# A decoder block's last row tiles: the row tile ahead of the last scaled on ScalarE and GpSimd instead of VectorE

## The chip, the core and the metric

The kernel runs on one core of a Trainium2 chip. Its time is the device time of one execution, in microseconds (us). A core has five engines with an in-order instruction stream each: TensorE (PE, matrix products into PSUM banks), VectorE (DVE), ScalarE (ACT), GpSimd (POOL) and SyncE (SP, which mostly issues DMA transfers). Engines meet only through semaphores. "Span" is the time from the first to the last instruction of the profiled execution.

## What is computed

One layer of a decoder block over 1024 tokens of width 1024, in float32: a mixer (a gated recurrence and a pooling branch), a layer norm, a squared-ReLU MLP and a second layer norm. Only the end matters here:

```python
x = layer_norm(DEEPNORM_ALPHA * x + mixer(x), ln1_g, ln1_b)
x = layer_norm(DEEPNORM_ALPHA * x + square(relu(x @ w_up)) @ w_down, ln2_g, ln2_b)

def layer_norm(x, g, b):
    mu  = mean(x);  var = mean(square(x - mu))
    return (x - mu) * rsqrt(var + 1e-5) * g + b
```

## The kernel before

A row tile is 128 tokens by 1024 features, and there are eight, numbered 0 to 7. Every float32 operand is split into a high and a low part, and each product is three matmuls (lines 1279 to 1281). The MLP's second product uses a Strassen-like scheme: seven products of half-size blocks, each added into one half (512 features) of four row tiles by `add_to` on VectorE (line 1235), which reads a PSUM bank and adds to the row tile `r[t]` in SBUF.

In the last block of the loop, the product `p5` completes row tiles 4 to 7, and after each of them `last_norm(t)` is called. The last two products, `p3` and `p2`, complete row tiles 0 to 3, and are issued interleaved by a list written out by hand, `(0, 0), (0, 1), (1, 0), (0, 2), (1, 1), (1, 2), (0, 3), (1, 3)`: first the product, then the row tile. So row tile 3 (`CH - 1`, with `CH` = 4) is the last to be finished, and row tile 2 (`CH - 2`) the one ahead of it. The adds and statistics of row tile 3 are given a higher priority. The order in which each engine's instructions finally stand is made by a scheduler at build time; the order in the source is only its input.

`last_norm(t)` works in four steps, and each line of it becomes one instruction, or one per half:

- statistics. For every row tile but the last, ScalarE sums the row (1307), turns the sum into minus the mean (1308), sums the squares around it (1309) and takes the root (1310). For row tile 3, VectorE's `bn_stats` (1042) runs after each half, then `bn_aggr` (1303), and ScalarE only takes the root (1304).
- first pass on VectorE (1315): `(r + minus mean) * g2`, in place.
- reciprocal of the root on VectorE, 128x1 (1316).
- second pass on VectorE (1318): `r * rstd + b2`, in place, then the DMA to the output (1319).

`parts` holds the slices that the passes run over: the whole row of 1024 for row tiles 0 to 2 and 4 to 7, two halves of 512 for row tile 3. The second `for` pairs each slice with a queue, the first with SP, the second with ScalarE's; with a whole row only SP is used. `g2` and `b2` are the norm's gain and bias, copied to all 128 partitions in SBUF (names `ln` in the profile); `mv` (name `lmv`) holds mean, root and reciprocal. Row tiles appear as `act` and, for row tile 7, `y`. GpSimd has issued the loads of the row tiles (1289) and computes nothing in this stage; its last elementwise work on whole row tiles is the bias add of the first layer norm (1062).

Of the kernel before, what the change touches and what calls it, by code (L numbers as in the profile page):

```python
# [12 lines left out]
AF = mybir.ActivationFunctionType  # L13
# [3 lines left out]
P = 128  # L17
# [6 lines left out]
CH = HALF // P  # L24
# [18 lines left out]
def tile_hybrid_block(  # L43
# [18 lines left out]
    nc = tc.nc  # L62
    V, A, G, PE = nc.vector, nc.scalar, nc.gpsimd, nc.tensor
    x2, out2 = x[0], out[0]
# [15 lines left out]
    def nm(s):  # L80
        seq[0] += 1
        return f"{s}_{seq[0]}"
# [38 lines left out]
    def split_into(t, src):  # L121
# [9 lines left out]
        out=cmask, in_=cmask, compare_op=ALU.is_ge, fill=0.0, base=0,  # L131
# [14 lines left out]
    r = [None] * 8  # L146
# [252 lines left out]
    with tc.tile_pool(name="xr", bufs=8, side="right", reuse_waits="tile") as xr:  # L399
# [68 lines left out]
        def parts(rows):  # L468
            return [split(row, row_tile) for row in rows]
# [62 lines left out]
        w = parts(b11)  # L532
        first_tokens("a12", "tr")
        onto_chain(w, "a11", True, copied(c11, c_late))
        with behind_parts("a11"):
            w = parts(b21)
        second_tokens("s3", "tr")
        by_rows(w, "a12", take_p2)
        with behind_parts("a12"):
            for k in range(CH):  # L540
                V.tensor_sub(b22[k], b22[k], b12[k])
            w = parts(b22)
# [3 lines left out]
        with behind_parts("s3"):  # L546
# [3 lines left out]
            w = parts(b21)  # L550
        second_tokens("s2")
        by_rows(w, "a22", take_p4)
        with behind_parts("a22"):
            w = parts(b22)
# [3 lines left out]
        with tc.issue_after(taken["a22", 1]):  # L558
            for k in range(CH):
                V.tensor_sub(b12[k], b12[k], b11[k])  # L560
            w = parts(b12)
# [7 lines left out]
        with behind_parts("s1"):  # L569
            w = parts(b22)  # L570
# [470 lines left out]
    def stats(t, cc, st):  # L1041
        V.bn_stats(st[:, cc], t[:, cc * HALF : (cc + 1) * HALF])
# [21 lines left out]
    def stat_tile():  # L1064
        return stat.tile([P, 2, 6], F32, tag="lst", name=nm("lst"), bufs=8)

    def ln_params(tile_of, *srcs):
        out = []
        for src in srcs:
            out.append(tile_of())  # L1070
            nc.scalar.dma_start(out=out[-1], in_=src.to_broadcast([P, D]))
        return out
# [5 lines left out]
    with tc.tile_pool(name="wo", bufs=1, side="right", reuse_waits="tile") as mp:  # L1078
        st1 = [None] * 8
        g1, b1 = ln_params(lambda: f(act_tile()).rearrange("p a b -> p (a b)"), ln1_g, ln1_b)  # L1080
        for k2 in range(0, KT, 2):
            raw = raw_rows(w_out, k2, 1)
            for k in range(2):
                n = len(wo)
# [47 lines left out]
    with tc.tile_pool(name="up", bufs=1, side="right", reuse_waits="tile") as up:  # L1132
# [96 lines left out]
        def add_to(t, n, ps):  # L1229
            y = r[t][:, n * HALF : (n + 1) * HALF]  # L1230
            if (t, n) not in touched:
                V.scalar_tensor_tensor(y, y, ALPHA, ps, ALU.mult, ALU.add)
                touched.add((t, n))
            else:
                V.tensor_add(y, y, ps)
# [38 lines left out]
        def down_tile(ops, chain, fresh, c):  # L1274
            ps = banks[1 - chain][c]
            w = slice(c * P, (c + 1) * P)
            for n in range(M):
                hh, hl, wh, wl = (t[:, n % 2] for t in ops[n // 2])
                PE.matmul(ps, hh[:, w], wh, start=fresh and n == 0, stop=False, skip_group_check=True)  # L1279
                PE.matmul(ps, hh[:, w], wl, start=False, stop=False, skip_group_check=True)  # L1280
                PE.matmul(ps, hl[:, w], wh, start=False, stop=n == M - 1, skip_group_check=True)  # L1281
            return ps
# [13 lines left out]
        for c, ps in done:  # L1296
            add_to(c, nh, ps)

    def last_norm(t):

        mv = stat.tile([P, 4], F32, tag="lmv", name=nm("lmv"), bufs=4)
        if t == CH - 1:
            V.bn_aggr(mv[:, 0:2], st1[t])
            A.activation(mv[:, 2:3], mv[:, 1:2], AF.Sqrt, bias=eps_ln)
        else:
            junk = dr.tile([P, D], F32, tag="junk", name=nm("junk"))
            A.activation(junk, r[t], AF.Copy, accum_out=mv[:, 3:4])
            A.activation(mv[:, 0:1], mv[:, 3:4], AF.Copy, scale=-1.0 / D)
            A.activation(junk, r[t], AF.Square, bias=mv[:, 0:1], accum_out=mv[:, 1:2])
            A.activation(mv[:, 2:3], mv[:, 1:2], AF.Sqrt, bias=eps_ln, scale=1.0 / D)  # L1310
        n = 2 if t == CH - 1 else 1
        parts = [slice(i, i + D // n) for i in range(0, D, D // n)]
        for w in parts:
            op = ALU.subtract if t == CH - 1 else ALU.add
            V.scalar_tensor_tensor(r[t][:, w], r[t][:, w], mv[:, 0:1], g2[:, w], op, ALU.mult)
        V.reciprocal(mv[:, 2:3], mv[:, 2:3])
        for w, eng in zip(parts, (nc.sync, nc.scalar)):
            V.scalar_tensor_tensor(r[t][:, w], r[t][:, w], mv[:, 2:3], b2[:, w], ALU.mult, ALU.add)
            eng.dma_start(out=out2[t * P : (t + 1) * P, w], in_=r[t][:, w])
# [5 lines left out]
    for b in range(NBLK):  # L1325
        if b:
            ws = ws_nxt
        last = b == NBLK - 1
        if last:

            for ring in (dh, dw):
                t = fw.tile([P, M, 2, HALF], F32R, tag="draw", name=nm("dx"), bufs=2)
                ring[:0] = [(t[:, n], t[:, n + 1]) for n in (0, 2)]
        for i, (name, slot, chain, fresh, (u, nh)) in enumerate(steps):
            if b == 0 and i == 0:
                continue
            if i == 2 and not last:
                ws_nxt = [(fw if b % 2 else dr).tile([P, M, D], F32, tag="draw", name=nm("draw"), bufs=2) for _ in range(2)]
                draws = down_rows(b + 1, ws_nxt)
            if i > 2 and not last and draws:  # L1340
                draws.pop(0)(h_load[0])
            if i == 2 and last:
                g2, b2 = ln_params(lambda: dr.tile([P, D], F32, tag="ln", name=nm("ln"), bufs=2), ln2_g, ln2_b)
            if last and name == "p3":
                break
            if b or i > 1:
                ops = down_operands(b, name, slot)
            for c in range(CH):
                t = u * CH + c
                add_to(t, nh, down_tile(ops, chain, fresh, c))  # L1350
                if last and name == "p5":
                    last_norm(t)
# [4 lines left out]
    for i, c in ((0, 0), (0, 1), (1, 0), (0, 2), (1, 1), (1, 2), (0, 3), (1, 3)):  # L1357
        _, _, chain, fresh, (_, nh) = ends[i]
        ps = down_tile(ops[i], chain, fresh, c)
        with tc.high_priority(PRIO) if c == CH - 1 else nullcontext():  # L1360
            add_to(c, nh, ps)
            if c == CH - 1:
                st1[c] = st1[c] if i else stat_tile()
                stats(r[c], nh, st1[c])
            if i:
                last_norm(c)


# [29 lines left out]
```

## Time and profile before

| what | value |
|---|---|
| time, median of 3 runs | 1460.14 us (1459.37 to 1463.32) |
| the profiled execution: its own time | 1462.62 us |
| the profiled execution: span | 1460.9 us |
| busy: DVE, ACT, POOL | 1137.3, 755.2, 60.5 us |
| last matmul starts | 1451.45 us |
| output issues after the last matmul | 1457.2 us (SP), 1457.91 us (ScalarE) |

Times in the profile are counted from the start of the span. Some 1.7 us of the profiled execution's own time lie outside its span. In a row of the timeline the columns are start, duration, engine, line, operation, output and inputs by name, shapes, and in brackets the idle time of the engine ahead of it with what ended it. In such a row the duration includes the drain of the pipeline, so the next instruction of the engine can start a little before the end. All times of this text refer to the kernel's line numbers before the change unless "changed kernel" is said; a suffix such as "row 2" means row tile 2.

### The profile page before, as it was taken

How to read it: one execution, taken by the hardware profiler on the slowest of the kernel's cores; microseconds unless marked ns; L12 is line 12 of the kernel's file. 1: busy time of each engine (PE TensorE's matmuls, PEld its weight loads, DVE VectorE, ACT ScalarE, POOL GpSimd, SP SyncE). 2: the span in 40 equal slices, each digit the busy share in tenths (PEclk: the TensorE clock that was granted, in tenths of full speed). 3: DMA queues.
4: the chain of work that ended last, by engine and by line, in shares of the span. 5: the costliest groups of instructions: out<-in, count | busy, mean ns of one | idle time of the engine just before them, and what ended most of it. 6: DMA issues, size and time to landing. Idle time of an engine off the chain costs nothing.

```text
span 1460.9 us, 20889 instructions
## 1 busy us (share of the span) xinstructions
PE 1438.2 (98%) x7505; PEld 1187.2 (81%) x7505; DVE 1137.3 (78%) x1838; ACT 755.2 (52%) x1381; POOL 60.5 (4%) x244
## 2 busy tenths in 40 slices
PE   9999999999999999999999999999999999999997
PEld 7888888888887887877788878888888888888886
DVE  5968989899997785768985597666666787777977
ACT  5545565665666566455442376555555443333535
POOL 0002010001001010000002100000000100000000
PEclk9999999999999999999999999999999999999999
DMA  7232233223333447987563225445464874444422
GB/s 252 77 118 88 85 104 114 82 94 103 103 121 116 152 133 236 334 285 249 193 224 119 73 94 195 146 141 170 142 242 155 288 260 152 151 137 167 129 72 116
DMA packets 160616, 226.84 MB, mean 155 GB/s; under 512 B 11232, under 2 KB 84480, under 8 KB 160512
## 3 DMA queue, kind: packets, MB, share of 16 engines
q1 hardware_dynamic: 158576, 218.93, 44.8%
q0 software_dynamic: 1152, 4.19, 0.9%
q10 hardware_dynamic: 784, 2.38, 0.5%
q8 instruction: 59, 0.97, 0.3%
q14 instruction: 45, 0.37, 0.1%
HBM read 154.16 MB, written 71.30 MB: 154 GB/s over the span
## 4 chain that ended last, share of the span: by engine, by line
PE 83%; DVE 7%; DMA 5%; ACT 3%; issue 2%; SPq 0%; DVEq 0%; ACTq 0%
PE ps_pj L199 14%; PE ps_pj L200 14%; PE ps_pj L201 14%; PE ps_pj L1280 4%; PE ps_pj L1281 4%; PE ps_pj L1279 4%; PE ps_pj L104 2%; PE ps_pj L105 2%; PE ps_pj L106 2%; DVE w L118 1%; PE ps_tr L1281 1%; PE ps_tr L1280 1%; PE ps_tr L1279 1%; PE ps_sc L199 1%; DMA draw<-in_w_down_dram 1%
## 5 line engine op out<-in xcount | busy, mean ns | idle before, releaser
L199 PE MATMUL ps_pj<-act,w 128*128 128x512 f32 x1068 | 419.8, 395 | 6.1 <-ACT w L117 3.1
L200 PE MATMUL ps_pj<-act,w 128*128 128x512 f32 x1068 | 417.7, 391 | 0.5 <-DVE act L123 0.5
L201 PE MATMUL ps_pj<-act,w 128*128 128x512 f32 x1068 | 412.0, 392 | 0.1
L199 PEld LDWEIGHTS ps_pj<-act,w 128*128 128x128 f32 x1068 | 200.8, 188 | 51.0 <-ACT w L117 4.9
L201 PEld LDWEIGHTS ps_pj<-act,w 128*128 128x128 f32 x1068 | 200.9, 188 | 43.2 <-DVE w L118 1.1
L200 PEld LDWEIGHTS ps_pj<-act,w 128*128 128x128 f32 x1068 | 201.1, 188 | 41.2 <-DVE act L123 0.9
L117 ACT CAST w<-t 128x512 fp32r<-128x512 f32 x170 | 104.9, 620 | 115.6 <-PE ps_pj L200 59.9
L118 DVE TENSOR_TENSOR w<-raw,w 128x512 fp32r<-128x512 f32 x143 | 99.1, 698 | 57.8 <-ACT w L117 43.7
L118 DVE TENSOR_TENSOR w<-t,w 128x512 fp32r<-128x512 f32 x170 | 115.9, 684 | 29.2 <-ACT w L117 27.5
L117 ACT CAST w<-raw 128x512 fp32r<-128x512 f32 x143 | 88.1, 620 | 89.4 <-PE ps_pj L200 39.7
L1241 ACT CAST act<-act 128x1024 fp32r<-128x1024 f32 x66 | 67.0, 1051 | 111.5 <-PE ps_pj L1280 36.1
L1280 PE MATMUL ps_pj<-act,act 128*128 128x512 f32 x240 | 93.3, 390 | 0.3 <-DVE act L1242 0.3
L1281 PE MATMUL ps_pj<-act,act 128*128 128x512 f32 x240 | 93.1, 389 | 0.0
L1279 PE MATMUL ps_pj<-act,act 128*128 128x512 f32 x240 | 92.4, 389 | 0.0
L1242 DVE TENSOR_TENSOR act<-act,act 128x1024 fp32r<-128x1024 f32 x66 | 79.3, 1219 | 16.1 <-ACT act L1241 16.0
L272 DVE TENSOR_TENSOR c<-c,ps_pj 128x512 f32<-128x512 f32 x95 | 64.5, 679 | 31.9 <-PE ps_pj L201 29.7
L268 ACT COPY c<-ps_pj 128x512 f32<-128x512 f32 x96 | 55.4, 584 | 15.4 <-PE ps_pj L201 14.8
L814 DVE RECIPROCAL tC<-tA 128x128 f32<-128x128 f32 x64 | 54.6, 906 | 0.0
L1280 PEld LDWEIGHTS ps_pj<-act,act 128*128 128x128 f32 x240 | 45.0, 188 | 10.1 <-DVE act L1242 0.7
L1279 PEld LDWEIGHTS ps_pj<-act,act 128*128 128x128 f32 x240 | 45.0, 188 | 9.4
L1281 PEld LDWEIGHTS ps_pj<-act,act 128*128 128x128 f32 x240 | 45.1, 188 | 9.2
L238 DVE TENSOR_TENSOR t<-raw,raw 128x512 f32<-128x512 f32 x43 | 29.5, 687 | 15.7 <-DMA raw<-in_w_in_dram 12.9
(415 smaller groups left out, 2721.0 us busy)
## 6 DMA issues: line engine op xcount, KB each, us to landing
h<-c SPq DMA_DIRECT2D x106, 256.0 KB, 2.3
act<-h SPq DMA_DIRECT2D x78, 256.0 KB, 3.0
raw<-in_w_in_dram SPq DMA_DIRECT2D x64, 256.0 KB, 3.4
draw<-in_w_down_dram SPq DMA_DIRECT2D x16, 1024.0 KB, 7.6
raw<-in_w_up_dram SPq DMA_DIRECT2D x30, 512.0 KB, 4.2
raw<-in_w_in_dram SPq DMA_DIRECT2D x18, 512.0 KB, 3.9
hf<-h SPq DMA_DIRECT2D x34, 256.0 KB, 2.9
c<-o SPq DMA_DIRECT2D x24, 256.0 KB, 4.2
```

Source lines behind the costliest of these rows:

```text
L117: A.copy(hi, src)
L118: V.tensor_sub(lo, src, f(hi))
L199: PE.matmul(ps, wh[:, k], th, start=first and k == 0, stop=False, skip_group_check=True)
L200: PE.matmul(ps, wh[:, k], tl, start=False, stop=False, skip_group_check=True)
L201: PE.matmul(ps, wl[:, k], th, start=False, stop=k == CH - 1, skip_group_check=True)
L268: A.copy(t, ps)
L272: V.tensor_add(t, t, ps)
L1241: A.copy(hi, src)
L1242: V.tensor_sub(lo, src, f(hi))
L1279: PE.matmul(ps, hh[:, w], wh, start=fresh and n == 0, stop=False, skip_group_check=True)
L1280: PE.matmul(ps, hh[:, w], wl, start=False, stop=False, skip_group_check=True)
L1281: PE.matmul(ps, hl[:, w], wh, start=False, stop=n == M - 1, skip_group_check=True)
```

## The change

Row tile 2 gets a path of its own inside `last_norm`. Its statistics stay. VectorE takes the reciprocal; ScalarE computes minus the mean times the reciprocal (128x1) and then, in two halves of 512, `r * rstd + that` in place; GpSimd multiplies each half by `g2`; GpSimd adds `b2` to the first half, and VectorE adds `b2` to the second. That last add is kept back in the list `ends_of` and issued behind the last call of `last_norm`. Both halves are sent from SP's queue.

The test for two parts is now `t >= CH - 2`. `last_norm` is also called for row tiles 4 to 7, so these too run in halves: eight passes of 1024 become sixteen of 512, and the second half of each of the four is sent from ScalarE's queue. Row tiles 0 and 1 stay whole, row tile 3 stays as it was.

```diff
+    ends_of = []
+
     def last_norm(t):
...
-        n = 2 if t == CH - 1 else 1
+        n = 2 if t >= CH - 2 else 1
         parts = [slice(i, i + D // n) for i in range(0, D, D // n)]
+        if t == CH - 2:
+            V.reciprocal(mv[:, 2:3], mv[:, 2:3])
+            A.activation(mv[:, 3:4], mv[:, 0:1], AF.Copy, scale=mv[:, 2:3])
+            for w in parts:
+                A.activation(r[t][:, w], r[t][:, w], AF.Identity, bias=mv[:, 3:4], scale=mv[:, 2:3])
+                G.tensor_mul(r[t][:, w], r[t][:, w], g2[:, w])
+            for w, eng in zip(parts, (G, V)):
+                def end(w=w, eng=eng):
+                    eng.tensor_add(r[t][:, w], r[t][:, w], b2[:, w])
+                    nc.sync.dma_start(out=out2[t * P : (t + 1) * P, w], in_=r[t][:, w])
+                end() if eng is G else ends_of.append(end)
+            return
...
             if i:
                 last_norm(c)
+    ends_of.pop()()
```

In the built program the order of TensorE's instructions is unchanged. VectorE's last instructions stand in this order: pass 2 of row 1, `bn_stats` of row 3, the reciprocal of row 2, the last add of row 3 from PSUM, `bn_stats`, `bn_aggr`, two halves of pass 1, reciprocal, two halves of pass 2, and the kept-back add of row 2. Pass 1 of row 0 stands behind the add of row 1 from PSUM, ahead of which it stood before. GpSimd's three instructions are its last. On SP the last three issues are the first half of row 3, GpSimd's half of row 2, VectorE's half of row 2.

## The prediction

> **What bounds the kernel now.** I read the page first, then the chain of waits over the last 35 us, then the timelines of VectorE, TensorE, ScalarE and GpSimd there, and last how GpSimd and VectorE get on elsewhere in the trace.
>
> ```profile
> PE 83%; DVE 7%; DMA 5%; ACT 3%; issue 2%; SPq 0%; DVEq 0%; ACTq 0%
> ```
>
> ```profile
> 1446.44 0.70 DVE act L1235
> 1447.13 1.28 DVE act L1315
> 1448.53 1.28 DVE act L1318
> 1449.81 0.60 DVE act L1235
> 1450.41 1.20 DVE act L1315
> 1451.68 0.59 DVE lst L1042
> 1452.27 0.59 DVE act L1235
> 1452.86 1.20 DVE act L1318
> 1454.05 0.62 DVE lst L1042
> 1454.94 1.41 DVE act L1315 x2
> 1456.46 0.75 DVE act L1318
> ```
>
> TensorE sets the pace nearly everywhere, and the change leaves its order alone. Only from 1446.44 does the chain run on VectorE: it still owes row 2 two wide passes (1450.41 and 1452.86, 1.20 us each) when row 3 is due. The change takes exactly these two away. So it can only act on some 15 us, and the question is what ends last there.
>
> **What the removal gives.** The steps, start to next start, are: add 0.60, wide pass 1.20, `bn_stats` 0.59, from the chain.
>
> ```profile
> 1443.72 0.69 DVE L1235 TENSOR_TENSOR act<-act,ps_sc 128x512 f32<-128x512 f32 x1
> 1452.19 0.67 DVE L1235 TENSOR_TENSOR act<-act,ps_tr 128x512 f32<-128x512 f32 x1
> 1454.69 0.21 DVE L1303 BATCH_NORM_AGGREGATE lmv<-lst 128x2 f32<-128x12 f32 x1
> 1454.94 1.41 DVE L1315 SCALAR_TENSOR_TENSOR act<-act,lmv,ln 128x512 f32<-128x512 f32 x2
> 1456.27 0.16 DVE L1316 RECIPROCAL lmv<-lmv 128x1 f32<-128x1 f32 x1
> 1456.46 1.41 DVE L1318 SCALAR_TENSOR_TENSOR act<-act,lmv,ln 128x512 f32<-128x512 f32 x2
> 1446.01 0.39 PE L1281 MATMUL ps_tr<-dx,dx 128*128 128x512 f32 x1
> 1448.73 0.39 PE L1281 MATMUL ps_pj<-act,act 128*128 128x512 f32 x1
> 1451.45 0.39 PE L1281 MATMUL ps_tr<-dx,dx 128*128 128x512 f32 x1
> ```
>
> An add follows the start of its last matmul by 0.43 us (1446.01 to 1446.44). From row 1's add at 1443.72, in the new order: row 0's pass 1 at 1444.32, reciprocal, pass 2 at 1445.72, row 2's add 1446.92, row 1's pass 1 1447.52, reciprocal, row 3's first add waiting for TensorE at 1448.73 + 0.43 = 1449.16, row 1's pass 2 1449.76, `bn_stats` 1450.96, row 2's reciprocal 1451.55. The last add then waits for TensorE, 1451.45 + 0.43 = **1451.88** (before: 1452.19). `bn_stats` 1452.47, aggregate 0.72 later at 1453.19, first half of pass 1 at **1453.44**, against 1454.94: 1.5 us gained so far.
>
> **What it adds, rows 4 to 7.** Two halves take 1.33 us (1454.94 to 1456.27) for a wide pass of 1.20: 0.13 us each, 8 x 0.13 = 1.06 us.
>
> ```profile
> 1441.00 0.69 DVE L1235 TENSOR_TENSOR act<-act,ps_pj 128x512 f32<-128x512 f32 x1 [0.17 <-PE ps_pj L1281]
> 1161.40 1.05 ACT L1241 CAST act<-act 128x1024 fp32r<-128x1024 f32 x1 [4.86 <-PE ps_pj L1280]
> 1161.76 0.33 ACTq L1071 DMA_DIRECT2D ln<-in_ln_g_dram  x1
> 1162.35 1.05 ACT L1241 CAST act<-act 128x1024 fp32r<-128x1024 f32 x1
> ```
>
> VectorE reached row 2's first add at 1440.83 and waited 0.17 us; it now comes at most 1.06 us later, 1441.9, is done by 1442.5 and waits for TensorE until 1443.72. That wait of 1.2 us is the cover: without it each 0.13 us would go through. Four DMA issues move from SP to ScalarE. An issue there takes 0.33 us beside the running instruction (the one at 1162.35 starts on time), so it costs nothing, but it waits for VectorE: row 7's, ready at about 1441.6 to 1441.9, holds up row 0's sum of squares until then; that is done about 1.5 us later, before 1443.5, and its user starts at 1444.32. I count this part as 0. If the cover were gone it would cost at most 1.06 us.
>
> **What it adds, row 2.** The reciprocal ends at 1451.70; then ScalarE needs 0.24 us for a 128x1 and twice a half pass, and GpSimd three instructions of 128x512, a form that has no row. They are bounded by 0.2 us (128x16) and 2.4 us (128x1024).
>
> ```profile
> L651 ACT ACTIVATE f<-f,lb,one_lb 128x512 f32<-128x512 f32 x16 | 13.1, 817 | 0.2
> L820 POOL TENSOR_TENSOR p<-T 128x16 f32<-128x16 f32 x16 | 3.6, 226 | 1.3
> L1062 POOL TENSOR_TENSOR r<-r,act 128x1024 f32<-128x1024 f32 x6 | 14.4, 2403 | 274.6 <-DVE r L1061 269.9 <-DVE lmv L1048 4.7
> ```
>
> A line through both gives (2403 - 226) / 1008 = 2.16 ns an element, so 226 + 496 x 2.16 = **1.30 us**, which I take; halving the nearer row gives 1.20. ScalarE's halves (817 ns) end at about 1452.80 and 1453.53, so GpSimd's first multiply runs from 1452.9 to 1454.2. If nothing else held, its three would end at 1456.8 and VectorE's own last add at 1456.97.
>
> The trace speaks against "nothing else held":
>
> ```profile
> 779.64 2.39 POOL L1062 TENSOR_TENSOR r<-r,act 128x1024 f32<-128x1024 f32 x1 [248.86 <-DVE r L1061]
> L118 DVE TENSOR_TENSOR w<-raw,w x2: 678/1591/2504, 780.1 to 782.5; 128x512 fp32r<-128x512 f32 x2
> ...
> 137.03 3.74 POOL L823 TENSOR_TENSOR p<-p 128x8 f32<-128x8 f32 x1
> 137.09 0.68 DVE L118 TENSOR_TENSOR w<-t,w 128x512 fp32r<-128x512 f32 x1
> ...
> 139.23 0.68 DVE L658 SCALAR_TENSOR_TENSOR q<-c,q 128x512 f32<-128x512 f32 x1
> ...
> 140.03 0.68 DVE L863 TENSOR_TENSOR tC<-tE,ek 128x512 f32<-128x512 f32 x1
> 140.64 2.56 DVE L814 RECIPROCAL tC<-tA 128x128 f32<-128x128 f32 x3
> 790.32 2.40 POOL L1062 TENSOR_TENSOR r<-r,act 128x1024 f32<-128x1024 f32 x1 [1.16 <-DVE r L1061]
> 790.87 0.69 DVE L1042 BATCH_NORM_STATS2 lst<-r 128x6 f32<-128x512 f32 x1
> ```
>
> While GpSimd worked from 779.64 to 782.03, a VectorE instruction with two SBUF inputs that started at 780.08 took 2504 ns (the longest of the two in its row: least, median, longest) where its twin took 678: it stood still until about 781.9. The other way round, a GpSimd instruction over 8 elements took 3.74 us, and came free when VectorE turned from a run of two-input instructions (the SCALAR_TENSOR_TENSOR among them) to a reciprocal. `bn_stats`, with one input, keeps its 0.69 us beside GpSimd. So the two exclude each other whenever VectorE reads two SBUF tensors, and both passes of row 3 (`r` with `g2`, `r` with `b2`) and the kept-back add are of that kind, while adds from PSUM and `bn_stats` are not.
>
> Then the end goes: pass 1's first half, due at 1453.44, stands until GpSimd's multiply is through, about 1454.05; halves at 1454.05 and 1454.72; reciprocal 1455.39. There GpSimd's second multiply gets in, 1455.45 to 1456.75, while pass 2 waits until 1456.6: halves at 1456.6 and 1457.3 (ending 1457.35 and 1458.0), kept-back add 1457.95 to 1458.65; only then GpSimd's add, 1458.65 to 1459.95. SP issues GpSimd's half at 1459.95 and, queued behind it though long ready, VectorE's half at 1460.3.
>
> The Trainium skill (SBUF — State Buffer, Who interferes with whom) says that whoever issues first has the shared ports for that whole instruction, and the other is blocked. The trace agrees on blocking, but its 3.74 us shows VectorE keeping them through a whole run of instructions. By the page's turns, one instruction each, the span would end at about 1463.8 (second rival); by the row, at about 1463.65.
>
> The transfers that follow:
>
> ```profile
> 1457.91 0.35 ACTq L1319 DMA_DIRECT2D out_dram<-act  x1
> ...
> 1458.00:1458.25 0.25, 0.00 (x0) 0.00 (x0) 0.00 (x0) 0.00 (x0) 0.00 (x0) 0.50 0.70 270
> ...
> 1459.50:1459.75 0.25, 0.00 (x0) 0.00 (x0) 0.00 (x0) 0.00 (x0) 0.00 (x0) 0.50 0.06 17
> ```
>
> In the kernel before, the half issued at 1457.2 starts moving at about 1458.05 (0.85 us later), the two halves of row 3 are through at about 1459.52, 0.73 us each, and the span ends 1.38 us after that. So: 1459.95 + 0.85 + 2 x 0.73 + 1.38 = 1463.64. **Sum: +2.75 us** against the span of 1460.9. The same execution would take 1462.62 + 2.75 = 1465.4; that execution lies 2.5 us over the median of the runs, so against the median it is 1460.14 + 2.75 = **1462.9 us**, 0.19% more.
>
> **The rivals.**
>
> *The engines don't exclude each other here* (this one ends on the other side). Place: GpSimd's three beside row 3's passes; point: whether pass 1's first half lasts 0.75 us or 1.3. Then row 3's halves leave at 1455.7 and 1456.4, GpSimd's and VectorE's at 1456.8 and 1457.1, data from 1456.55, and four halves of 0.73 us make 1459.5, as before: the transfer takes the whole gain, and the time is 1460.1. If only the last half counted, 1457.1 + 0.85 + 0.73 + 1.38 = 1460.1 in the span, 0.8 less, 1459.3; I take 1459.8. For it: no row has exactly this pair of forms. Against it: 2504 and 3741 ns above.
>
> *GpSimd gets in earlier.* If it keeps its turn through all three, to 1456.75, row 3's passes start then, its first half leaves at 1458.9, and four halves from 1459.8 end at 1462.7, span 1464.1, +3.2: 1463.3 us. If the two alternate by single instructions, row 3's first half leaves at 1458.6, data runs from 1459.45 to 1462.4, span 1463.8, +2.9: 1463.0. For it: its next instruction is waiting when one ends. Against: VectorE had asked earlier.
>
> *GpSimd's halves cost as much as whole rows,* 2.4 us, nothing saved by halving. Three of them, each 1.1 us over my value, all on the chain: +2.75 + 3.3, about 1466.2 us. Against: the line through the two sizes.
>
> *It does other than it says,* since the test also halves rows 4 to 7: up to 1.06 us more if the cover fails, 1463.9. Against: the 1.2 us of waiting left.
>
> **How the numbers follow.** Forecast with exclusion in VectorE's order 0.55, GpSimd in earlier 0.20, no exclusion 0.15, GpSimd at full-row price 0.04, rows 4 to 7 showing 0.06. The first two give 1462.9 to 1463.3. Bounds: no exclusion 1459.3 to 1460.1 below; above, 1463.9 for the rows, and the runs of before alone spread over 4 us, so the range is 1459.6 to 1465.3. A measurement of this kernel can tell about 0.3% (4.4 us) from no change: the forecast is well inside. Over it lie the full-row price, and a forecast pushed up by the runs' spread, together 0.15; faster by as much has no case, 0.01.
>
> **What would show it.** Right: pass 1's first half of row 3 stretched to about 1.3 us, pass 2's first likewise, a GpSimd instruction stretched where VectorE has its run, the last two issues on SP near 1460 and 0.34 us apart, last add from PSUM at 1451.9. Wrong: 0.75 us halves beside busy GpSimd (first rival); GpSimd's 128x512 far from 1.3 us; a last add later than 1452.2 (rows 4 to 7 or row 0 are late); TensorE's last matmul elsewhere than 1451.45.

## The result and the profile after

The changed kernel takes 1462.25 us (median of 22 runs, 1460.66 to 1464.71), the kernel before 1460.24 us (22 runs, 1457.33 to 1463.32). The ratio is 1.0014, 95% interval 1.0008 to 1.0020: slower by 2.0 us, between 1.2 and 2.9. That is inside the 0.3% that the prediction took as the least that can be told from no change, though over 22 runs of each the difference is clear of zero.

The head of the page of the changed kernel:

```profile
span 1460.1 us, 20911 instructions
...
PE 1434.5 (98%) x7505; PEld 1184.7 (81%) x7505; DVE 1139.0 (78%) x1845; ACT 757.0 (52%) x1384; POOL 65.8 (5%) x247
```

The profiled execution took 1461.8 us, and its span is 0.8 us *shorter* than that of before (1460.9), against the verdict of the runs. The reason is where TensorE is when the end begins: here the last matmul starts at 1448.15, before at 1451.45. In the eleven kernels of this study it starts anywhere from 1447.98 to 1451.45, with and without the change, and TensorE's order is the same in before and after. So spans of single executions can't be subtracted. In both traces TensorE runs without a gap from 1424 us to its last matmul, so the change doesn't hold it up, and what the change costs can only show behind it. What can be subtracted is therefore the **tail**, from the start of the last matmul to the end of the span: 9.45 us before, 11.95 us after, **+2.5 us**. Below, "+x" is a time after the start of the last matmul.

The chain that ended last, in the changed kernel (start, duration, what):

```profile
1448.57 0.70 DVE act L1235
...
1450.27 2.87 DVE act L1330 x2
1453.14 0.08 DVE lmv L1331
...
1453.25 1.56 DVE act L1333
```

VectorE still sets the end, but through other instructions. Row 2's wide passes are gone, and pass 1 of row 3 (two halves) now lasts 2.87 us where it lasted 1.41; the first half of pass 2 lasts 1.56 instead of 0.75. The timeline of TensorE, VectorE, GpSimd and the two output queues shows with what they collide:

```profile
1448.15 0.39 PE L1281 MATMUL ps_tr<-dx,dx 128*128 128x512 f32 x1
1448.57 0.69 DVE L1235 TENSOR_TENSOR act<-act,ps_tr 128x512 f32<-128x512 f32 x1 [0.17 <-PE ps_tr L1281]
...
1449.66 1.26 POOL L1321 TENSOR_TENSOR act<-act,ln 128x512 f32<-128x512 f32 x1 [288.10 <-ACT act L1320]
1450.27 1.20 DVE L1330 SCALAR_TENSOR_TENSOR act<-act,lmv,ln 128x512 f32<-128x512 f32 x1
1450.89 1.70 POOL L1321 TENSOR_TENSOR act<-act,ln 128x512 f32<-128x512 f32 x1
1451.40 1.75 DVE L1330 SCALAR_TENSOR_TENSOR act<-act,lmv,ln 128x512 f32<-128x512 f32 x1
1452.55 1.71 POOL L1324 TENSOR_TENSOR act<-act,ln 128x512 f32<-128x512 f32 x1
1453.25 1.56 DVE L1333 SCALAR_TENSOR_TENSOR act<-act,lmv,ln 128x512 f32<-128x512 f32 x1
1454.73 0.74 DVE L1333 SCALAR_TENSOR_TENSOR act<-act,lmv,ln 128x512 f32<-128x512 f32 x1
...
1454.84 0.33 SPq L1334 DMA_DIRECT2D out_dram<-act  x1
1455.27 0.37 SPq L1325 DMA_DIRECT2D out_dram<-act  x1
1455.39 0.68 DVE L1324 TENSOR_TENSOR act<-act,ln 128x512 f32<-128x512 f32 x1
1455.50 0.34 ACTq L1334 DMA_DIRECT2D out_dram<-act  x1
1456.10 0.33 SPq L1325 DMA_DIRECT2D out_dram<-act  x1
```

Read the durations as a zip. Undisturbed, a half of row 3's passes has 0.75 us in its row. GpSimd's first multiply is undisturbed (1.26 us). VectorE's first half asks at 1450.27 and lasts 1.20, because that multiply runs until 1450.92; GpSimd's second multiply lasts 1.70, because that half runs; VectorE's second half lasts 1.75, because of that multiply; GpSimd's add lasts 1.71, and VectorE's next half 1.56. From VectorE's first half on, each engine waits for one instruction of the other, then gets its own. Only when GpSimd has nothing left do VectorE's instructions return to 0.74 and 0.68. The waits on VectorE are 1.20 - 0.75 = 0.45, 1.75 - 0.75 = 1.00 and 1.56 - 0.75 = 0.81, together 2.26 us.

The transfers, in windows of the same execution (the last two columns are the share of the DMA engines and GB/s):

```profile
1455.50:1456.00 0.50, 0.00 (x0) 0.00 (x0) 0.50 (x1) 0.00 (x0) 0.00 (x0) 0.50 0.63 238
...
1458.25:1458.50 0.25, 0.00 (x0) 0.00 (x0) 0.00 (x0) 0.00 (x0) 0.00 (x0) 0.50 0.69 254
1458.50:1458.75 0.25, 0.00 (x0) 0.00 (x0) 0.00 (x0) 0.00 (x0) 0.00 (x0) 0.50 0.01 0
```

Filling 0.63 of the first window and 0.69 of the second, data moves from about 1455.68 to 1458.43 without a gap (the windows between them are filled to 0.99 or more). Such readings are good to a few hundredths of a us. In the tails:

| step | before | after | difference |
|---|---|---|---|
| first half of row 3 issued | +5.76 | +6.69 | +0.93 |
| first data moves | +6.60 | +7.53 | |
| last data through | +8.07 (2 halves, 1.47 us) | +10.28 (4 halves, 2.75 us) | +1.28 more |
| end of span | +9.45 (1.38 later) | +11.95 (1.67 later) | +0.29 more |

So the loss has two main parts and a small one. VectorE asks for row 3 earlier (+2.12, before +3.49), but the waits of 2.26 us turn these 1.37 us of gain into 0.9 of loss; and behind row 3 now stand row 2's two halves as well, which were out earlier before. The last 0.29 us lie behind the last data; e1 and e2 below show what they go with.

### The profile page after: what moved, and what is told of

Its sections match the earlier page's. It is cut to its first block, busy times and chain, and to the rows that moved or that the text cites. A ratio compares the mean times of both kernels' runs of the same rounds, so it can differ in the third digit from the quotient of the medians.

```text
span 1460.1 us, 20911 instructions
## 1 busy us (share of the span) xinstructions
PE 1434.5 (98%) x7505; PEld 1184.7 (81%) x7505; DVE 1139.0 (78%) x1845; ACT 757.0 (52%) x1384; POOL 65.8 (5%) x247
## 4 chain that ended last, share of the span: by engine, by line
PE 86%; DMA 5%; DVE 4%; ACT 2%; issue 1%; SPq 0%; DVEq 0%; ACTq 0%
PE ps_pj L199 14%; PE ps_pj L200 14%; PE ps_pj L201 14%; PE ps_pj L1280 4%; PE ps_pj L1279 4%; PE ps_pj L1281 4%; PE ps_pj L105 2%; PE ps_pj L106 2%; PE ps_pj L104 2%; PE ps_tr L1280 1%; PE ps_tr L1279 1%; PE ps_tr L1281 1%; PE sc L887 1%; PE ps_sc L199 1%; PE ps_sc L200 1%
```

## The experiments

The theory after the result: GpSimd and VectorE exclude each other by single instructions, in turns, when both read SBUF and VectorE reads two tensors there; with it, row 2's output is put into the last queue. The rivals: rows 4 to 7 in halves cost the time; the transfers alone do; VectorE's instructions are stretched by something else, such as the pointer scalars that they read. All runs in one table; the ratio is to the kernel before on the same chip.

| kernel | tail, us | last issue | time ratio, 95% interval |
|---|---|---|---|
| before | 9.45 | +6.46 | |
| after | 11.95 | +7.95 | 1.0014 (1.0008 to 1.0020) |
| e1: rows 4 to 7 whole again | 10.92 | +7.17 | 1.0010 (1.0001 to 1.0019) |
| e2: before, rows 4 to 7 in halves | 10.32 | +7.08 | 1.0005 (0.9994 to 1.0016) |
| e3: GpSimd only writes | 9.67 | +5.69 | 1.0003 (0.9995 to 1.0012) |
| e4: gain and bias from PSUM | 9.63 | +5.77 | 1.0002 (0.9993 to 1.0011) |
| e5: before, GpSimd at work beside it | 11.30 | +8.27 | 1.0019 (1.0010 to 1.0028) |
| e6: before, row 2 sent last | 10.72 | +6.76 | 1.0005 (0.9996 to 1.0014) |
| e7: gain and bias from PSUM, row 2 on GpSimd alone | 9.38 | +6.50 | 0.9997 (0.9988 to 1.0005) |
| e9: e5 without pointer scalars | 11.01 | +7.97 | one run: 1461.4 us |
| e10: reciprocal of row 2 earlier | 11.79 | +7.78 | 1.0019 (1.0010 to 1.0028) |

The tails and the ratios agree: a tail that is d us longer than before should give a ratio of 1 + d/1460, and each of the nine timed rows has that inside its interval. The tail is that of one execution, without an interval of its own. By time alone e2, e3, e4, e6 and e7 can't be told from the kernel before; what follows rests on the rows of the traces.

**e3 and e4: is it the reading of SBUF?** In e3 GpSimd's three instructions become six that only write, and the kept-back add stays on VectorE. It leaves out row 2's gain and the bias of its first half, and overwrites the values:

```diff
-                G.tensor_mul(r[t][:, w], r[t][:, w], g2[:, w])
+                for _ in range(2):
+                    G.memset(r[t][:, w], 1.0)
...
-                    eng.tensor_add(r[t][:, w], r[t][:, w], b2[:, w])
+                    for _ in range(2 if eng is G else 0):
+                        G.memset(r[t][:, w], 1.0)
+                    if eng is V:
+                        V.tensor_add(r[t][:, w], r[t][:, w], b2[:, w])
```

> The changed kernel with each of GpSimd's three operations on row 2 replaced by two memsets of the same half (GpSimd writes and reads nothing; row 2's gain, and the bias of its first half, are left out). GpSimd is busy about as long (six times 0.53 us). Theory (the exclusion is about reading two SBUF tensors on VectorE against a reading GpSimd): all four half passes of row 3 take 0.75 us, its first half leaves 4.4 us after the last matmul against 6.7 in the changed kernel; four halves of 0.7 us follow, last matmul to end 9.3 to 9.7 us, time within 0.5 us of before. Rival (any GpSimd work or the semaphores slow the passes): halves stay at 1.2 to 1.7 us, 11.9 us.

VectorE's passes of row 3, and two of the GpSimd instructions beside them:

```profile
1451.15 1.41 DVE L1334 SCALAR_TENSOR_TENSOR act<-act,lmv,ln 128x512 f32<-128x512 f32 x2
1452.67 1.42 DVE L1337 SCALAR_TENSOR_TENSOR act<-act,lmv,ln 128x512 f32<-128x512 f32 x2
...
1452.04 0.53 POOL L1326 MEMSET act<- 128x512 f32 x1
1452.50 0.53 POOL L1322 MEMSET act<- 128x512 f32 x1
```

Both passes have the length they had before (1.41), beside a busy GpSimd. A GpSimd that is at work is no trouble here; one that reads SBUF is. The tail drops from 11.95 to 9.67.

e4 leaves GpSimd as it is in the change and moves the second operand of VectorE's passes instead: ScalarE copies `g2` and `b2` into four PSUM banks that have come free, and row 3's passes and the kept-back add read them there.

```diff
-            V.scalar_tensor_tensor(r[t][:, w], r[t][:, w], mv[:, 0:1], g2[:, w], op, ALU.mult)
+            V.scalar_tensor_tensor(r[t][:, w], r[t][:, w], mv[:, 0:1], gw, op, ALU.mult)
...
+            if (i, c) in ((0, 0), (0, 1), (1, 0), (0, 2)):
+                n_in = len(in_psum)
+                src = (g2, b2)[n_in // 2][:, n_in % 2 * HALF : (n_in % 2 + 1) * HALF]
+                A.copy(ps, src)
+                in_psum.append(ps)
```

> The changed kernel, but row 3's passes and VectorE's add for row 2 read g2 and b2 from four PSUM banks that are free by then (four ScalarE copies of 0.58 us while it idles), so that VectorE reads one SBUF tensor each. GpSimd's work is unchanged. Theory: all half passes 0.75 us beside a busy GpSimd whose three take 1.1 to 1.3 us each; first half leaves 4.4 us after the last matmul; last matmul to end 9.3 to 9.7 us, time within 0.5 us of before, 2 us under the changed kernel. Rival (VectorE is slowed by GpSimd whatever it reads): halves 1.2 to 1.7 us, 11.9 us.

```profile
1452.19 1.41 DVE L1333 SCALAR_TENSOR_TENSOR act<-act,lmv,ps_pj 128x512 f32<-128x512 f32 x2
1453.71 0.75 DVE L1336 SCALAR_TENSOR_TENSOR act<-act,lmv,ps_hg 128x512 f32<-128x512 f32 x1
...
1451.59 2.49 POOL L1324 TENSOR_TENSOR act<-act,ln 128x512 f32<-128x512 f32 x2 [288.67 <-ACT act L1323]
1454.04 1.26 POOL L1327 TENSOR_TENSOR act<-act,ln 128x512 f32<-128x512 f32 x1
```

The same three GpSimd instructions (1.26 us each, unstretched) now lie beside VectorE's passes (0.75 us a half, unstretched). This is the cause shown from both sides: take away GpSimd's reads (e3) or VectorE's second SBUF operand (e4), and the waits of 2.26 us are gone. The tail falls by 2.32 us, to 9.63. The Trainium skill (SBUF — State Buffer, Who interferes with whom) has both exceptions: a VectorE instruction with two SBUF inputs contends only with a GpSimd instruction that reads SBUF, and one with a single SBUF input doesn't contend, outside the modes in which it uses two ports. Both runs agree: the two halves of a pass take 1.40 to 1.42 us in each.

e4 also shows that without the exclusion the change still wins nothing: its pass 1 starts at +2.12 instead of +3.49, and its tail is 0.18 us longer than before's, its timed ratio 0.9993 to 1.0011.

**e6: what do the transfers cost alone?** The kernel before, with row 2 sent in two halves behind row 3's first half:

```diff
+            if t == CH - 2:
+                continue
...
+    for w in (slice(0, HALF), slice(HALF, D)):
+        with tc.issue_after(sent[0].ins):
+            nc.sync.dma_start(out=out2[(CH - 2) * P : (CH - 1) * P, w], in_=r[CH - 2][:, w])
```

> The kernel before with row 2's output sent as two halves behind row 3's first half on SP; no engine's arithmetic changes. Theory (four half transfers of 0.7 us at the end instead of two): data from 1458.05 on for 2.8 us instead of 1.47, last matmul to end about 10.8 us, time +1.35 us. Rival (the loss comes from the ports alone): 9.45 us, time as before.

SP's and ScalarE's queues at the end:

```profile
1453.77 0.33 SPq L1323 DMA_DIRECT2D out_dram<-act  x1
1454.16 0.91 SPq L1375 DMA_DIRECT2D out_dram<-act  x2
1454.44 0.35 ACTq L1323 DMA_DIRECT2D out_dram<-act  x1
```

VectorE is that of before (row 3's first half leaves at +5.79, before +5.76), and the tail is 1.27 us longer. That is the 1.28 us of the table above: the transfer's part of the loss. It is read from one trace; the timed ratio, 0.9996 to 1.0014, holds it and holds 1 as well.

**e5 and e9: GpSimd beside the kernel before.** In e5 a copy of one column on GpSimd waits for `bn_aggr` of row 3, and three multiplies of 128x512 on a scratch tile follow; nobody uses their output.

```diff
...
+            G.tensor_copy(idle[:, 0:1], mv[:, 0:1])
+            for _ in range(3):
+                G.tensor_mul(idle[:, :HALF], idle[:, :HALF], g2[:, :HALF])
```

> The kernel before with three extra GpSimd multiplies 128x512 (two SBUF inputs, result unused) that start right behind row 3's aggregate; nothing else changes, and the transfers stay two halves at the end. Theory, turns by single instructions: VectorE's first half pass runs, then GpSimd and VectorE alternate, and the three later half passes wait 1.05, 0.85 and 1.05 us: last matmul to end about 12.4 us, time +2.9 us. Theory, VectorE keeps the ports through a run: only pass 2's first half waits, about +0.85 us, 10.3 us. Rival (the loss of the changed kernel comes from transfers alone): 9.45 us, time as before.

```profile
1452.88 1.42 DVE L1320 SCALAR_TENSOR_TENSOR act<-act,lmv,ln 128x512 f32<-128x512 f32 x2
1454.41 3.23 DVE L1323 SCALAR_TENSOR_TENSOR act<-act,lmv,ln 128x512 f32<-128x512 f32 x2
...
1452.98 0.70 POOL L1306 COPY idle<-lmv 128x1 f32<-128x1 f32 x1 [4.47 <-DVE lmv L1303]
1453.77 4.99 POOL L1308 TENSOR_TENSOR idle<-idle,ln 128x512 f32<-128x512 f32 x3
```

The tail of 11.30 lies between the two figures that were expected. The reason is in the third line: the little copy itself waited behind VectorE (0.70 us), so the multiplies came late and met only pass 2. There the halves waited 3.23 - 1.42 = 1.81 us, more than one GpSimd instruction of 1.26 us can make them wait, so both did: VectorE didn't keep GpSimd out through its two halves. Since GpSimd's instructions here serve nobody, e5 also shows the exclusion alone, with no row 2 behind it: the tail is 1.85 us longer.

e9 repeats e5 with constants in place of the pointer scalars (the mean and the reciprocal, 128x1 each) in row 3's passes; it leaves out row 3's normalisation. It was to tell theory A, that VectorE gives way because it reads `mv`, from theory B, that it gives way after every instruction.

```diff
+                    behind.append(V.scalar_tensor_tensor(r[t][:, w], r[t][:, w], 0.25, g2[:, w], ALU.subtract, ALU.mult))
...
+                    behind.append(V.scalar_tensor_tensor(r[t][:, w], r[t][:, w], 0.5, b2[:, w], ALU.mult, ALU.add))
```

> As the run with three extra GpSimd multiplies beside the kernel before, but row 3's four half passes take constants in place of the mean and the reciprocal (128x1 tensors), so row 3's normalisation is left out. There pass 2's two halves took 3.23 us against 1.41, that is, each half let GpSimd in between. Theory A (between two VectorE instructions GpSimd gets the ports only where the next one first loads a 128x1 scalar; without it a run of VectorE keeps them, as in the 3.74 us row): only pass 2's first half waits, pass 2 takes about 2.3 us, and the 128x1 copy on GpSimd waits for both halves of pass 1, 1.3 us instead of 0.70. Theory B (turns by single instructions always): 3.2 us and 0.7 us as there.

```profile
1452.06 1.24 DVE L1321 SCALAR_TENSOR_TENSOR act<-act,ln 128x512 f32<-128x512 f32 x2
1453.29 3.34 DVE L1326 SCALAR_TENSOR_TENSOR act<-act,ln 128x512 f32<-128x512 f32 x2
...
1452.27 0.47 POOL L1306 COPY idle<-lmv 128x1 f32<-128x1 f32 x1 [4.47 <-DVE lmv L1303]
```

Pass 2 is stretched as in e5 (3.34 us; A expected 2.3, B 3.2), and the copy took 0.47 us (A expected 1.3, B 0.7). Theory A falls, B stands.

**e2 and e1: rows 4 to 7.** The prediction priced their halving at nothing. e2 is the kernel before with that part alone:

```diff
-        n = 2 if t == CH - 1 else 1
+        n = 2 if t >= CH - 1 else 1
```

> Only the halving of row tiles 4 to 7, row 2 as before. Theory: no difference, last matmul to end 9.45 us, time within 0.5 us of before. Rival (halving costs): up to 1.06 us more, 10.5 us.

```profile
1449.48 0.39 PE L1281 MATMUL ps_tr<-dx,dx 128*128 128x512 f32 x1
1450.85 0.67 DVE L1235 TENSOR_TENSOR act<-act,ps_tr 128x512 f32<-128x512 f32 x1
```

The last add starts at +1.37; before it was +0.74 (1452.19 against 1451.45). These 0.63 us reach the last output issue (+7.08 against +6.46), and the tail is 0.87 us longer, near the rival's figure. Not because the halves are slower: behind them VectorE still waits 1.65 us for TensorE, at row 1's last add. But in the built program pass 1 of row 0 has moved behind that add, and pass 2 of row 1 behind row 3's first add, so VectorE comes late to what follows. The time ratio, 0.9994 to 1.0016, neither shows nor excludes it.

The other 0.25 us of e2 or so lie behind the last data. From there to the end of the span it is 1.61 to 1.67 us in the five kernels that halve rows 4 to 7 (the change, e2, e3, e4, e10), and 1.33 to 1.47 us in the six that leave them whole (before, e1, e5, e6, e7, e9). So the change's 0.29 us there go with the halving; by what means isn't shown.

e1 is the changed kernel with rows 4 to 7 whole again; the order of the last adds and issues is pinned to that of the change (lines left out here).

```diff
-        n = 2 if t >= CH - 2 else 1
+        n = 2 if t in (CH - 2, CH - 1) else 1
```

> The change without the halving of row tiles 4 to 7 (these stay whole, all on SP); row 2 on ScalarE and GpSimd as in the changed kernel, its kept-back add and its two transfers behind row 3's by explicit order. Theory (GpSimd and VectorE exclude each other beside row 3's passes, and four half transfers instead of two stand at the end): as the changed kernel, last matmul to end of span 11.9 us against 9.45 before, time +2.0 us. Rival (halving rows 4 to 7 costs): up to 1.06 us less than the changed kernel, 10.9 us from last matmul to end.

```profile
1449.68 0.39 PE L1281 MATMUL ps_tr<-dx,dx 128*128 128x512 f32 x1
1448.57 0.16 DVE L1317 RECIPROCAL lmv<-lmv 128x1 f32<-128x1 f32 x1
1451.80 2.90 DVE L1335 SCALAR_TENSOR_TENSOR act<-act,lmv,ln 128x512 f32<-128x512 f32 x2
1454.81 1.41 DVE L1338 SCALAR_TENSOR_TENSOR act<-act,lmv,ln 128x512 f32<-128x512 f32 x2
...
1449.99 2.49 POOL L1321 TENSOR_TENSOR act<-act,ln 128x512 f32<-128x512 f32 x2 [287.27 <-ACT act L1320]
```

The tail is 1.03 us shorter than the change's, as the rival had it. But pass 1 is asked at +2.12, as in the change: VectorE wasn't late there. What is earlier is row 2's reciprocal, at -1.11 instead of +0.11, and with it GpSimd, so that pass 2 is free of it (1.41) and the waits are 1.49 us instead of 2.26. These 0.77 us and the 0.24 us less behind the last data (1.43 against 1.67) make up 1.01 of the 1.03.

**e10: is it that reciprocal?** The change as it is, with row 3's first `bn_stats` behind row 2's reciprocal instead of ahead of it, and the end pinned as in e1:

```diff
-                stats(r[c], nh, st1[c])
+                with tc.issue_after(ready[0].ins) if not i else nullcontext():
+                    stats(r[c], nh, st1[c])
```

> The changed kernel with one VectorE instruction moved: row 2's reciprocal ahead of row 3's first bn_stats, so that GpSimd begins 0.6 us earlier (0.9 us after the last matmul instead of 1.5); the kept-back add and row 2's transfers stand behind row 3's as in the changed kernel. Theory (the later GpSimd begins, the more of its three meet row 3's passes; halving rows 4 to 7 cost its 1.0 us this way, since with whole rows GpSimd began at 0.3 us): the passes lose 0.4 to 0.6 us less to waiting, 1.7 to 1.85 us in place of 2.26, last matmul to end about 11.4 us. Rival (the halves of rows 4 to 7 cost in another way, by ScalarE's issues or SP's queue): 11.95 us as the changed kernel.

```profile
1452.04 3.50 DVE L1335 SCALAR_TENSOR_TENSOR act<-act,lmv,ln 128x512 f32<-128x512 f32 x2
1455.65 1.42 DVE L1338 SCALAR_TENSOR_TENSOR act<-act,lmv,ln 128x512 f32<-128x512 f32 x2
1450.84 2.48 POOL L1321 TENSOR_TENSOR act<-act,ln 128x512 f32<-128x512 f32 x2 [287.99 <-ACT act L1320]
```

GpSimd started at +0.93, 0.58 us earlier than in the change, as expected, but the tail is 11.79, not about 11.4: only 0.16 us won. Pass 1 was asked at 1452.04, just as GpSimd's first multiply ended (1450.84 + 1.26 = 1452.10), and the second multiply went first: the two together last 2.48 us, unstretched, and pass 1's halves waited 3.50 - 1.41 = 2.09 us. In e1 pass 1 was asked at 1451.80, in the middle of GpSimd's second multiply, so less of it was left to wait for. By these rows an earlier GpSimd helps or not by where its turns happen to fall against VectorE's first request; that is read from three traces and not tested further.

**e7: is there a version that wins?** e4, with rows 4 to 7 whole, row 2's reciprocal early, row 2's last add on GpSimd too, and its first half sent ahead of row 3's:

```diff
+            for w in parts:
+                with tc.issue_after(in_pool[-1].ins) if in_pool else nullcontext():
+                    G.tensor_mul(r[t][:, w], r[t][:, w], g2[:, w])
+                    in_pool.append(G.tensor_add(r[t][:, w], r[t][:, w], b2[:, w]))
```

> A version meant to keep the gain: rows 4 to 7 whole; row 2's reciprocal ahead of row 3's first statistics; GpSimd does all of row 2's gain and bias, half by half, and each half is sent when ready, the first ahead of row 3's; row 3's passes read gain and bias from PSUM. Theory (no exclusion left, only the last three halves wait for each other in the transfers): all half passes 0.75 us, GpSimd's four 1.26 us each from 0.6 us after the last matmul, its last end at 5.6 us; last matmul to end 8.7 to 8.9 us against 9.45 before, time 0.6 us under before (near what the runs can resolve). Rival (something else takes the gain): 9.5 us or more.

```profile
1450.62 1.26 POOL L1326 TENSOR_TENSOR act<-act,ln 128x512 f32<-128x512 f32 x1 [287.75 <-ACT act L1323]
...
1454.54 1.26 POOL L1327 TENSOR_TENSOR act<-act,ln 128x512 f32<-128x512 f32 x1
```

GpSimd began at +1.30, not at +0.6, and four instructions of 1.26 us end at +6.48; its half is issued at +6.50, the last of all. The tail is 9.38 where 8.7 to 8.9 was expected, 0.07 us shorter than before, and the ratio's interval holds 1. GpSimd had taken VectorE's place as the bound. No version here is measurably faster than the kernel before.

## Why the prediction was right, and where not

The forecast was 1462.9 us; 1462.25 was measured, +2.0 us (1.2 to 2.9) against +2.75 predicted. The sign held, and so did the outline of the mechanism: GpSimd and VectorE exclude each other, and row 2's transfers come last. Two steps of the way failed, and that the size came out so near is in part luck: their errors nearly cancel, as the item on the transfers shows.

- **What bounds the end**: right. VectorE in the last stretch; the last add came 0.42 us after the last matmul (0.43 predicted), pass 1 was asked at +2.12 (predicted +1.99), so 1.37 us earlier than before (predicted 1.5).
- **TensorE's last matmul at 1451.45**: it came at 1448.15. By the prediction's own list that was a sign of error, but kernels with and without the change spread over the same 3.5 us; the list should have named the tail.
- **GpSimd's 128x512**: right. 1.26 us against 1.30; the rival with 2.4 us falls. It began at +1.51 (predicted +1.45).
- **The exclusion**: right, and shown by e3 and e4. The rival "the engines don't exclude each other" falls. Its other half, that the transfer takes the whole gain, was true: e4's tail is 9.63 against 9.45.
- **Who gets the next turn**: wrong. The failed step is "VectorE keeping them through a whole run", taken from the 3.74 us row. VectorE gave way after single instructions: three of its four halves waited (0.45, 1.00 and 0.81 us), where the forecast let the first half of each pass wait, and GpSimd's add went in ahead of pass 2, not behind the kept-back add. GpSimd's half was ready at 1454.26 (+6.11; predicted +8.5), and the last issue came at +7.95 (predicted +8.85). The second branch of the rival "GpSimd gets in earlier" had the order: alternation by single instructions. The Trainium skill (SBUF — State Buffer, Who interferes with whom) gives the ports to whoever issues first, for that whole instruction. The 1.20, 1.70, 1.75, 1.71 and 1.56 us here agree; who comes next when both have more to do the section doesn't say, so "the page's turns" was a reading of it. That branch gave +2.9 us where the tail shows +2.5: its first half of row 3 left at +7.15, in the trace at +6.69.
- **The transfers**: the terms held (0.84 us from issue to data where 0.85 was counted, 0.69 us a half where 0.73 was), but four halves stood in the queue, 2.75 us, where the forecast had the last two count, 1.46 us, because it had GpSimd's half come so late. The forecast's end lies at +12.19, the trace's at +11.95. The issue from which the last transfers count came 1.81 us earlier (row 3's first half at +6.69, where the forecast counted from GpSimd's half at +8.50), the queue was 1.29 us longer, and the stretch behind the last data 0.29 us: these errors come to some -0.24 us. No step of the prediction foresaw this cancelling.
- **Rows 4 to 7 at nothing**: wrong by the traces. The cover held as described, and the last add was not late in the change. But the zero looked only at the covered stretch. e1 and e2 put the part at 1.03 and 0.87 us of tail: in e2 by the order that the scheduler then makes, in the change against e1 by longer waits on GpSimd, and in both by some 0.25 us behind the last data; not by the 0.13 us of a half. It is within the prediction's bound of 1.06 us (8 x 0.13 is 1.04), and the timed runs don't separate it from zero.

## What to carry to other kernels

Before giving GpSimd elementwise work beside VectorE, count VectorE's instructions there with two SBUF operands: each can wait for one GpSimd instruction that reads SBUF (up to 1.00 us of its 1.26 in the change), and reading one operand from PSUM took that away here. Work that is taken off the last engine still has to leave through the last queue, so add its transfer to the end before counting a gain. Compare ends of profiles from the last event that the change can't move, not by spans.

## What the runs showed of the hardware that was not expected

The waits here lie inside the instructions' durations, not ahead of them, and they are gone in e3 and e4: the engines meet at more than the semaphores that the opening names. Between back-to-back instructions GpSimd and VectorE took turns one by one (1.20, 1.70, 1.75, 1.71, 1.56 us in the change), with and without pointer scalars. The row on which the forecast leaned, a GpSimd instruction over 8 elements that took 3.74 us beside a run of VectorE's two-input instructions, doesn't fit turns, and stays unexplained. In e10 GpSimd's next instruction went ahead of a VectorE pass that asked at 1452.04, about the moment at which the first one ended (1452.10), and the pass took 3.50 us. GpSimd instructions of 0.53 us that only write ran beside two-input passes at no cost to those (1.41 and 1.42 us).
